# First FFN split in two parts, with Strassen's scheme for 19 of its 22 tiles

## The chip, the cores and the metric

The kernel runs on one core of one Trainium2 chip. The metric is device time in microseconds (us), the median of several runs. Engines are named as in the profile: PE (TensorE), DVE (VectorE), ACT (ScalarE), POOL (GpSimd), SP (SyncE, which here only issues transfers).

## The reference

One layer over 512 latent tokens and 256 context tokens, model width 1024, in float32. Nine vectors of modulation per token kind come from one product with `w_mod`. FFN 1 (both token kinds), attention with pooling, and FFN 2 (latent tokens alone) follow each other.

```python
def swiglu(h, w_gu, w_down):
    a, b = jnp.split(h @ w_gu, 2, axis=-1)        # width 2 x 2816
    return (jax.nn.silu(a) * b) @ w_down
...
    ml = jnp.split(mod_lat, N_MOD, axis=-1)       # silu(c) @ w_mod + b_mod
    lat = lat + 0.5 * ml[2] * swiglu(modulate(rms_norm(lat, g_norm[layer, 0]), ml[0], ml[1]),
                                     w_ffn_gu[layer, 0], w_ffn_down[layer, 0])
    cx = cx + 0.5 * mc[2] * swiglu(modulate(rms_norm(cx, g_norm[layer, 0]), mc[0], mc[1]),
                                   w_ffn_gu[layer, 0], w_ffn_down[layer, 0])
...
    lat = lat + ml[5] * branch_merge(attn_lat, pool_lat, gates_l, ...)
    lat = lat + 0.5 * ml[8] * swiglu(modulate(rms_norm(lat, g_norm[layer, 2]), ml[6], ml[7]),
                                     w_ffn_gu[layer, 1], w_ffn_down[layer, 1])
return rms_norm(lat, g_final)
```

## The kernel before

**Products.** Every float32 operand is kept as a high and a low part (`split`, L121 on ACT and L122 on DVE). A product is three matmuls (`mm3`): high times high (L138), high times low (L139), low times high (L141). A weight tile of 128 x 1024 is loaded by SP (`weights`), split, and used from a ring of four.

**FFN 1.** The hidden width 2816 is 22 tiles of 128 (j). `Hidden` makes one tile: gate and up, each over 8 blocks of 128 input rows (kt), for 512 latent and 256 context columns. ACT applies Silu, DVE multiplies gate and up (L407), and the product is split and stays on chip. After each group of tiles (`CHUNKS`: 4, 4, 4, 4, 2, 4) `ffn_down` projects the group back: for each of 8 output blocks i, the tiles of the group are multiplied into two PSUM banks, and DVE adds the result to the residual streams xo and xc (L544). So gate, up and down alternate. There are 7 PSUM banks in a ring and one for the totals below.

**Modulations.** Vectors 0 and 1 are needed at the start. `Mod` makes vectors 2 to 8 beside FFN 1: for each block kt of the condition, `step` loads rows of `wm` on POOL's queue (1 MB for two blocks, two buffers) and DVE adds them, scaled, to an accumulator macc (L250; the first by L252). The vectors 2 to 4 have two accumulators, one for each token kind, 5 to 8 one. `total` sums over the partitions by matmuls on PE (acc, L260), and `finish` brings the vector into place. The steps are handed out between the tiles.

**FFN 2** has 4 plain tiles and 18 tiles by Strassen's scheme: `Quad` takes gate and up of one tile as a 2 x 2 block product over two halves of 4 kt and two halves of 256 tokens, in seven products of 4 kt instead of eight. The sums of weight blocks are made by DVE (L450, L451) and POOL (L453, L454), and split. `HalfSums` makes the four sums of token blocks once, t0 to t3, one for each pair of kt (POOL adds high and low, L509; DVE differences, L513).

**Order.** The program is written as if it ran in sequence. A scheduler sets the order of the instructions on each engine; each engine then runs its own queue in order, and semaphores hold an instruction until its inputs are there.

Of the kernel before, what the change touches and what calls it, by code (L numbers as in the profile page):

```python
# [97 lines left out]
def tile_layer(ctx: ExitStack, tc: tile.TileContext, a: dict, out: bass.AP):  # L98
# [259 lines left out]
    hl = [hp.tile([P, 2, SEQ], F32R, name=f"hl{k}") for k in range(KT)]  # L358
    def stream_tile():
        t = xo.tile([P, KT, SEQ], F32, name="xo")  # L360
        return t, [t[:, k, :] for k in range(KT)]

    xl_all, xl = stream_tile()
    hctx_stack = ExitStack()
    hcp = pool("hcp", hctx_stack, bufs=1, side="right")
    HCW = CTX + 8
    hc_new = lambda: [hcp.tile([P, 2, HCW], F32R, name=f"hc{k}")[:, :, 0:CTX] for k in range(KT)]
    hc = hc_new()
# [870 lines left out]
```

## Time and profile before

| | us |
|---|---|
| median of 3 runs | 1494.99 (1494.97 to 1495.32) |
| the profiled execution, its own time | 1496.38 |
| its span | 1494.6 |
| PE busy | 1458.3 |
| DVE busy | 951.1 |
| ACT busy | 602.1 |
| POOL busy | 327.9 |

The span is the time from the first to the last instruction of the profiled execution. The busy times are sums over the whole span; the stretches differ from each other: FFN 1 runs to about 580 us, FFN 2 begins at about 1130 us. The granted clock of PE is 0.997 of full speed over the span.

### The profile page before, as it was taken

How to read it: one execution, taken by the hardware profiler on the slowest of the kernel's cores; microseconds unless marked ns; L12 is line 12 of the kernel's file. 1: busy time of each engine (PE TensorE's matmuls, PEld its weight loads, DVE VectorE, ACT ScalarE, POOL GpSimd, SP SyncE). 2: the span in 40 equal slices, each digit the busy share in tenths (PEclk: the TensorE clock that was granted, in tenths of full speed). 3: DMA queues.
4: the chain of work that ended last, by engine and by line, in shares of the span. 5: the costliest groups of instructions: out<-in, count | busy, mean ns of one | idle time of the engine just before them, and what ended most of it. 6: DMA issues, size and time to landing. Idle time of an engine off the chain costs nothing.

```text
span 1494.6 us, 22635 instructions
## 1 busy us (share of the span) xinstructions
PE 1458.3 (98%) x9280; PEld 1301.5 (87%) x9280; DVE 951.1 (64%) x1423; ACT 602.1 (40%) x989; POOL 327.9 (22%) x239
## 2 busy tenths in 40 slices
PE   6999999999999999989999999999999999999998
PEld 4888888888888889979999988888899799989997
DVE  5678468433233237677767677633487978879786
ACT  5321121221221225666666666422356434434343
POOL 1000001000000013544545555000144422212210
PEclk9999999999999999999999999999999999999999
DMA  9445368312112122310101111433353323233231
GB/s 377 163 156 183 113 226 280 129 57 71 57 57 73 37 64 71 128 57 29 57 30 57 35 66 50 141 99 92 106 169 120 93 85 113 86 113 114 85 99 57
DMA packets 41497, 156.69 MB, mean 105 GB/s; under 512 B 4657, under 2 KB 4913, under 8 KB 37425
## 3 DMA queue, kind: packets, MB, share of 16 engines
q1 hardware_dynamic: 36640, 124.76, 25.4%
q0 software_dynamic: 4032, 29.36, 5.4%
q8 instruction: 73, 1.20, 0.3%
q10 hardware_dynamic: 720, 1.11, 0.2%
q14 instruction: 32, 0.25, 0.1%
HBM read 151.03 MB, written 4.19 MB: 104 GB/s over the span
## 4 chain that ended last, share of the span: by engine, by line
PE 87%; DVE 7%; ACT 2%; issue 2%; POOL 1%; DMA 0%; DVEq 0%; SPq 0%; ACTq 0%; POOLq 0%
PE ps L138 26%; PE ps L139 26%; PE ps L141 26%; PE sc L877 1%; PE sc L876 1%; PE ps L901 1%; PE ps L785 1%; PE ps L786 1%; PE ps L787 1%; DVE w_lo L122 1%; DVE tmp L301 1%; DVE tmp L323 1%; DVE e L887 1%; DVE tmp L513 1%; ACT w_hi L121 1%
## 5 line engine op out<-in xcount | busy, mean ns | idle before, releaser
L121 ACT ACTIVATE w_hi<-w_raw 128x1024 fp32r<-128x1024 f32 (+1 forms) x213 | 210.2, 988 | 591.2 <-PE ps L139 317.8
L138 PE MATMUL ps<-hl,w_hi 128*128 128x512 f32 (+1 forms) x880 | 324.8, 372 | 0.8 <-DVE xo L913 0.4
L139 PE MATMUL ps<-hl,w_hi 128*128 128x512 f32 (+1 forms) x880 | 322.1, 367 | 0.0
L141 PE MATMUL ps<-hl,w_lo 128*128 128x512 f32 (+1 forms) x880 | 321.8, 367 | 0.0
L122 DVE TENSOR_TENSOR w_lo<-w_raw,w_hi 128x1024 fp32r<-128x1024 f32 (+1 forms) x175 | 210.3, 1202 | 133.9 <-ACT w_hi L121 133.2
L122 POOL TENSOR_TENSOR w_lo<-w_raw,w_hi 128x1024 fp32r<-128x1024 f32 x38 | 93.0, 2449 | 504.8 <-ACT w_hi L121 474.0
L138 PE MATMUL ps<-act_hi,w_hi 128*128 128x512 f32 (+1 forms) x592 | 200.7, 339 | 0.1
L139 PE MATMUL ps<-act_lo,w_hi 128*128 128x512 f32 (+1 forms) x592 | 192.3, 335 | 0.0
L138 PEld LDWEIGHTS ps<-hl,w_hi 128*128 128x128 f32 x880 | 165.6, 189 | 29.7 <-issue 2.2
L141 PEld LDWEIGHTS ps<-hl,w_lo 128*128 128x128 f32 x880 | 165.8, 189 | 13.5 <-issue 0.4
L139 PEld LDWEIGHTS ps<-hl,w_hi 128*128 128x128 f32 x880 | 166.1, 189 | 11.6 <-DVE hl L330 0.3
L141 PE MATMUL ps<-act_hi,w_lo 128*128 128x512 f32 (+1 forms) x592 | 174.0, 337 | 1.6 <-DVE w_lo L122 1.6
L139 PE MATMUL ps<-hc,w_hi 128*128 128x256 f32 (+1 forms) x484 | 136.5, 282 | 0.0
L141 PE MATMUL ps<-hc,w_lo 128*128 128x256 f32 (+1 forms) x484 | 135.6, 281 | 0.0
L138 PE MATMUL ps<-hc,w_hi 128*128 128x256 f32 (+1 forms) x484 | 135.6, 282 | 0.0
L138 PEld LDWEIGHTS ps<-act_hi,w_hi 128*128 128x128 f32 x592 | 111.7, 189 | 19.2 <-issue 0.8
L139 PEld LDWEIGHTS ps<-act_lo,w_hi 128*128 128x128 f32 x592 | 111.8, 189 | 11.9
L544 DVE SCALAR_TENSOR_TENSOR xo<-ps,mods,xo 128x512 f32<-128x512 f32 (+1 forms) x112 | 74.3, 670 | 70.2 <-PE ps L141 70.1
L141 PEld LDWEIGHTS ps<-act_hi,w_lo 128*128 128x128 f32 x592 | 102.3, 190 | 8.7 <-DVE w_lo L122 3.1
L138 PEld LDWEIGHTS ps<-hc,w_hi 128*128 128x128 f32 x484 | 90.7, 188 | 16.5 <-ACT hc L329 0.2
L139 PEld LDWEIGHTS ps<-hc,w_hi 128*128 128x128 f32 x484 | 91.1, 188 | 15.6 <-issue 0.2
L250 DVE SCALAR_TENSOR_TENSOR macc<-wm,cond,macc 128x1024 f32<-128x1024 f32 x70 | 88.7, 1280 | 6.8 <-DMA wm<-in_wm 6.1
(252 smaller groups left out, 2847.1 us busy)
## 6 DMA issues: line engine op xcount, KB each, us to landing
w_raw<-in_gu SPq DMA_DIRECT2D x88, 512.0 KB, 3.5
wm<-in_wm POOLq DMA_DIRECT2D x28, 1024.0 KB, 5.2
w_raw<-in_dn SPq DMA_DIRECT2D x40, 512.0 KB, 3.6
w_raw<-in_wi SPq DMA_DIRECT2D x36, 512.0 KB, 3.5
wm<-in_wm SPq DMA_DIRECT2D x16, 512.0 KB, 10.9
w_raw<-in_wo SPq DMA_DIRECT2D x16, 512.0 KB, 3.5
w_raw<-in_wv SPq DMA_DIRECT2D x8, 512.0 KB, 3.5
w_raw<-in_wa SPq DMA_DIRECT2D x8, 512.0 KB, 3.4
```

The lines of the kernel that those rows point to most:

```text
L121: nc.scalar.activation(out=hi, in_=src, func=AF.Copy)
L122: (lo_engine or nc.vector).tensor_tensor(out=lo, in0=src, in1=f32(hi), op=ALU.subtract)
L138: nc.tensor.matmul(out=o, lhsT=wh, rhs=ah, start=start, stop=False)
L139: nc.tensor.matmul(out=o, lhsT=wh, rhs=al, start=False, stop=False)
L141: nc.tensor.matmul(out=o, lhsT=wl, rhs=ah, start=False, stop=stop)
L250: nc.vector.scalar_tensor_tensor(out=acc, in0=wm, scalar=c, in1=acc, op0=ALU.mult, op1=ALU.add)
L301: nc.vector.tensor_tensor(out=acc, in0=acc, in1=sq, op=ALU.add)
L323: nc.vector.scalar_tensor_tensor(out=t, in0=x, scalar=scale, in1=r, op0=ALU.mult, op1=ALU.mult)
L513: sub = lambda out, x, y, op=ALU.subtract: nc.vector.tensor_tensor(out=out, in0=x, in1=y, op=op)
L544: nc.vector.scalar_tensor_tensor(out=xa, in0=po, scalar=mod(gate_i, i, s), in1=xa, op0=ALU.mult, op1=ALU.add)
L785: nc.tensor.matmul(out=o, lhsT=hh, rhs=vh, start=(kt == 0), stop=False)
L786: nc.tensor.matmul(out=o, lhsT=hh, rhs=vl, start=False, stop=False)
```

## The change

- The first three tiles of FFN 1 (`PLAIN1`) stay plain, with two spans of 384 columns instead of 512 and 256. Latent and context tokens lie side by side in one tile of 768 columns (hb).
- Tiles 3 to 21 are `Quad`s over halves of 384 tokens, with `HalfSums` over hb. The weight sums have two buffers instead of the three of FFN 2.
- The product of gate and up of every tile, 128 x 768, goes to DRAM (`store_act`, on POOL's queue). After the last quad the pools of this part are closed; x and the context are loaded again (8 transfers of SP).
- Then `ffn_down` runs for groups of 2, 5, 8, 3 and 4 tiles (`ACT_CHUNKS`). Their activations come back through `Stored`: one load by SP, and a split into two tiles. The group of two is loaded during the last quads.
- A step of `Mod` loads 512 KB for one kt instead of 1 MB for two. Modulations 2 to 4 run beside the quads, with one wm buffer; their steps are called twice in each quad. Modulations 5 to 8 run beside the down projections, two steps for each output block, with two wm buffers.

```diff
 CHUNKS = (4, 4, 4, 4, 2, 4)
+ACT_CHUNKS = (2, 5, 8, 3, 4)
+PLAIN1 = 3
...
         def step(self, kt):
-            if kt % 2 == 0:
-                self.wm = self.pool.tile([P, 2, D], F32, name="wm")
-                if self.after is not None:
-                    nc.gpsimd.tensor_copy(out=self.wm[:, 0, 0:1], in_=self.after)
-                nc.gpsimd.dma_start(out=self.wm, in_=a["wm"][self.i - 2, kt // 2])
+            wm = self.pool.tile([P, D], F32, name="wm")
+            nc.gpsimd.dma_start(out=wm, in_=a["wm"][self.i - 2, kt // 2, :, kt % 2])
             if kt == 0:
-                self.acc = [self.pool.tile([P, D], F32, name="macc", bufs=3) for _ in self.streams]
+                self.acc = [self.pool.tile([P, D], F32, name="macc", bufs=2) for _ in self.streams]
...
+    class Stored:
...
+            raw = raw_pool.tile([P, ALL], F32, name="act_raw")
+            nc.sync.dma_start(out=raw, in_=src)
...
+            split(lat_tile[:, 0, :], lat_tile[:, 1, :], raw[:, 0:SEQ])
+            split(ctx_tile[:, 0, :], ctx_tile[:, 1, :], raw[:, SEQ:ALL])
...
-    both = [(hl, 0, SEQ), (hc, 0, CTX)]
+    HALF = ALL // 2
+    both = [(hb, 0, HALF), (hb, HALF, HALF)]
...
+    def store_act(j, gate):
+        nc.gpsimd.dma_start(out=act_dram[j], in_=gate)
...
+    modp1 = pool("modp1", right_stack, bufs=1, side="right")
...
+    sums1 = HalfSums(hb, HALF, tq1, row)
+    quads1 = {j: Quad(w_gu1, j, wq1, 2, cq1, sums1, row, lambda q, gate: store_act(q.j, gate)) for j in range(PLAIN1, NJ)}
...
+    todo = [lambda k=k: sums1.build(k) for k in range(HK)]
+    for h_ in first[2:]:
+        for part in range(2):
+            h_.products(part, range(KT // 2))
+            if todo:
+                todo.pop(0)()
...
+    def add_mods(idx, pool_):
+        for i in idx:
+            m = Mod(i, pool_, (LAT, CX) if i < 5 else (LAT,))
+            pending.extend([lambda m=m, kt=kt: m.step(kt) for kt in range(KT)] + [m.total, m.finish])
...
+    add_mods((2, 3, 4), modp1)
+    stored = []
+    for j, qd in quads1.items():
+        qd.all(next_pending)
...
+    for k in range(0, KT, 2):
+        nc.sync.dma_start(out=xl_all[:, k:k + 2], in_=a["xT"][:, k:k + 2])
+        nc.sync.dma_start(out=xc_all[:, k:k + 2], in_=a["cT"][:, k:k + 2])
...
+    modp = pool("modp", ffn_stack, bufs=2)
+    add_mods((5, 6, 7, 8), modp)
...
+    two = lambda: (next_pending(), next_pending())
...
+        following = bring(starts[c + 1], nj, c + 1 != 2)
+        run(ffn_down(w_dn1, starts[c], acts, every), {i: two for i in range(KT)})
+        acts = following
```

Two places in the order of the instructions. The first is DVE while the third tile of FFN 1 and its neighbours are on PE. Before, the steps of modulation 2 (macc) stand between low parts of weights (w_lo) and of activations (act_lo):

```order
L250 SCALAR_TENSOR_TENSOR macc_716<-wm_722,cond_83,macc_716 128x1024
L250 SCALAR_TENSOR_TENSOR macc_717<-wm_722,cond_83,macc_717 128x1024
L122 TENSOR_TENSOR w_lo_923<-w_raw_921,w_hi_922 128x1024
L122 TENSOR_TENSOR act_lo_702<-tmp_703,act_hi_701 128x512
L122 TENSOR_TENSOR act_lo_702<-tmp_708,act_hi_701 128x256
L250 SCALAR_TENSOR_TENSOR macc_716<-wm_853,cond_83,macc_716 128x1024
L250 SCALAR_TENSOR_TENSOR macc_717<-wm_853,cond_83,macc_717 128x1024
L122 TENSOR_TENSOR w_lo_993<-w_raw_991,w_hi_992 128x1024
L250 SCALAR_TENSOR_TENSOR macc_716<-wm_853,cond_83,macc_716 128x1024
L250 SCALAR_TENSOR_TENSOR macc_717<-wm_853,cond_83,macc_717 128x1024
L250 SCALAR_TENSOR_TENSOR macc_716<-wm_916,cond_83,macc_716 128x1024
L407 TENSOR_TENSOR tmp_843<-tmp_843,ps_791 128x512
```

After the change the same stretch of DVE's queue is the end of the block sums: differences (gate from up, L516), steps of modulation 2 (macc_1002, macc_1003) and the low parts of t2 and t3, on which the first quad's matmuls wait.

```order
L516 TENSOR_TENSOR gate_847<-up_845,gate_847 128x384
L249 SCALAR_TENSOR_TENSOR macc_1003<-wm_1317,cond_74,macc_1003 128x1024
L516 TENSOR_TENSOR gate_848<-up_845,gate_847 128x384
L124 TENSOR_TENSOR t2_657<-gate_847,t2_657 128x768
L516 TENSOR_TENSOR gate_885<-up_881 128x384
L124 TENSOR_TENSOR t2_657<-gate_848,t2_657 128x768
L516 TENSOR_TENSOR gate_885<-up_883,gate_885 128x384
L516 TENSOR_TENSOR gate_886<-up_881,up_883 128x384
L249 SCALAR_TENSOR_TENSOR macc_1002<-wm_1425,cond_74,macc_1002 128x1024
L249 SCALAR_TENSOR_TENSOR macc_1003<-wm_1425,cond_74,macc_1003 128x1024
L516 TENSOR_TENSOR gate_886<-up_883,gate_885 128x384
L124 TENSOR_TENSOR t3_658<-gate_885,t3_658 128x768
```

The steps of modulation 2 have moved in between the block sums.

The second is the total of modulation 5. On PE before, it stands between two tiles of gate and up (ps from hl and hc):

```order
L139 MATMUL ps_2352<-hl7_110,w_hi_2347 128x512
L138 MATMUL ps_2353<-hc7_122,w_hi_2347 128x256
L139 MATMUL ps_2353<-hc7_122,w_hi_2347 128x256
L141 MATMUL ps_2352<-hl7_110,w_lo_2348 128x512
L141 MATMUL ps_2353<-hc7_122,w_lo_2348 128x256
L260 MATMUL acc_2402<-macc_2083,half_100 32x256 x4
L138 MATMUL ps_2415<-hl0_103,w_hi_2410 128x512
L139 MATMUL ps_2415<-hl0_103,w_hi_2410 128x512
```

On DVE its last step (macc_2083) stands in a piece between low parts, some tiles ahead:

```order
L122 TENSOR_TENSOR w_lo_1955<-w_raw_1953,w_hi_1954 128x1024
L250 SCALAR_TENSOR_TENSOR macc_2083<-wm_2148,cond_83,macc_2083 128x1024 x2
L250 SCALAR_TENSOR_TENSOR macc_2083<-wm_2270,cond_83,macc_2083 128x1024 x2
L407 TENSOR_TENSOR tmp_1796<-tmp_1796,ps_1744 128x512
L407 TENSOR_TENSOR tmp_1801<-tmp_1801,ps_1745 128x256
L122 TENSOR_TENSOR w_lo_2021<-w_raw_2019,w_hi_2020 128x1024
L122 TENSOR_TENSOR act_lo_1795<-tmp_1796,act_hi_1794 128x512
L122 TENSOR_TENSOR act_lo_1795<-tmp_1801,act_hi_1794 128x256
L250 SCALAR_TENSOR_TENSOR macc_2083<-wm_2342,cond_83,macc_2083 128x1024 x2
L122 TENSOR_TENSOR w_lo_2088<-w_raw_2086,w_hi_2087 128x1024
```

After the change the total (acc_3793) stands on PE between output blocks of the first down group (act_a are its two activations):

```order
L143 MATMUL ps_3778<-act_a_3076,w_lo_3773 128x256
L140 MATMUL ps_3778<-act_a_3083,w_hi_3772 128x256
L141 MATMUL ps_3778<-act_a_3083,w_hi_3772 128x256
L143 MATMUL ps_3778<-act_a_3083,w_lo_3773 128x256
L259 MATMUL acc_3793<-macc_3694,half_91 32x256 x4
L268 MATMUL ps_3800<-ident_63,tmp_3798 128x4 x2
L140 MATMUL ps_3804<-act_a_3076,w_hi_3772 128x512
L141 MATMUL ps_3804<-act_a_3076,w_hi_3772 128x512
```

On DVE the steps of modulation 5 (macc_3694) stand in front of the residual update of the next output block (L563, ps_3804), the first three of modulation 6 (macc_3822) too:

```order
L249 SCALAR_TENSOR_TENSOR macc_3694<-wm_3715,cond_74,macc_3694 128x1024
L249 SCALAR_TENSOR_TENSOR macc_3694<-wm_3718,cond_74,macc_3694 128x1024
L124 TENSOR_TENSOR hl1_3890<-act_raw_3892,hl1_3890 128x512
L249 SCALAR_TENSOR_TENSOR macc_3694<-wm_3743,cond_74,macc_3694 128x1024
L249 SCALAR_TENSOR_TENSOR macc_3694<-wm_3746,cond_74,macc_3694 128x1024
L249 SCALAR_TENSOR_TENSOR macc_3694<-wm_3765,cond_74,macc_3694 128x1024
L249 SCALAR_TENSOR_TENSOR macc_3694<-wm_3768,cond_74,macc_3694 128x1024
L251 TENSOR_SCALAR macc_3822<-wm_3820,cond_74 128x1024
L271 TENSOR_TENSOR mods_90<-ps_3800,vecs_64 128x8
L249 SCALAR_TENSOR_TENSOR macc_3822<-wm_3824,cond_74,macc_3822 128x1024
L249 SCALAR_TENSOR_TENSOR macc_3822<-wm_3849,cond_74,macc_3822 128x1024
L563 SCALAR_TENSOR_TENSOR xo_3616<-ps_3804,mods_90,xo_3616 128x512
```

On POOL the loads of these steps follow the last activation stores:

```order
L649 DMA act20_219<-gate_3382 128x768
L649 DMA act21_220<-gate_3489 128x768
L243 DMA wm_3692<-in_wm 128x1024
L243 DMA wm_3696<-in_wm 128x1024
L243 DMA wm_3715<-in_wm 128x1024
L243 DMA wm_3718<-in_wm 128x1024
```

The last step, the total and the down projections behind it now stand within one group.

## Rows read from the trace of the kernel before

**Rows 1.** The page: busy time, GB/s by fortieth, chain that ended last
```profile
PE 1458.3 (98%) x9280; PEld 1301.5 (87%) x9280; DVE 951.1 (64%) x1423; ACT 602.1 (40%) x989; POOL 327.9 (22%) x239
...
GB/s 377 163 156 183 113 226 280 129 57 71 57 57 73 37 64 71 128 57 29 57 30 57 35 66 50 141 99 92 106 169 120 93 85 113 86 113 114 85 99 57
...
PE 87%; DVE 7%; ACT 2%; issue 2%; POOL 1%; DMA 0%; DVEq 0%; SPq 0%; ACTq 0%; POOLq 0%
```

**Rows 2.** Busy us by stretch: length, PE, PEld, DVE, ACT, POOL, clock, DMA, GB/s
```profile
30.00:120.00 90.00, 90.00 (x605) 75.29 (x604) 62.40 (x83) 28.73 (x45) 8.19 (x12) 1.00 0.54 193
120.00:400.00 280.00, 280.00 (x1634) 241.70 (x1634) 151.06 (x187) 52.08 (x78) 10.55 (x20) 1.00 0.40 138
...
1147.00:1185.00 38.00, 36.40 (x216) 32.23 (x215) 37.53 (x49) 18.75 (x31) 17.93 (x9) 1.00 0.26 84
...
1200.00:1480.00 280.00, 279.90 (x1986) 263.61 (x1986) 237.39 (x343) 114.79 (x153) 56.59 (x32) 1.00 0.30 95
```

**Rows 3.** Timeline of PE near 704 us: start, us, instruction
```profile
704.08 0.34 PE L876 MATMUL sc<-k,q 128*128 128x384 f32 x1
704.25 0.33 PE L877 MATMUL sc<-k,ql 128*128 128x384 f32 x1
704.42 0.33 PE L876 MATMUL sc<-k,q 128*128 128x384 f32 x1
704.60 0.28 PE L138 MATMUL ps<-pa_hi,v_hi 128*128 128x256 f32 x1
704.72 0.28 PE L139 MATMUL ps<-pa_lo,v_hi 128*128 128x256 f32 x1
```

**Rows 4.** Timeline of DVE near 55 us: last normalised block of FFN 1
```profile
54.44 0.74 DVE L330 SCALAR_TENSOR_TENSOR hl<-tmp,mods,hl 128x512 fp32r<-128x512 f32 x1
55.10 0.47 DVE L330 SCALAR_TENSOR_TENSOR hc<-tmp,mods,hc 128x256 fp32r<-128x256 f32 x1
```

**Rows 5.** DVE by line and form: count, busy us, mean ns, idle before
```profile
L122 DVE TENSOR_TENSOR w_lo<-w_raw,w_hi 128x1024 fp32r<-128x1024 f32 x140 | 185.9, 1328 | 118.8 <-ACT w_hi L121 118.3
L250 DVE SCALAR_TENSOR_TENSOR macc<-wm,cond,macc 128x1024 f32<-128x1024 f32 x70 | 88.7, 1280 | 6.8 <-DMA wm<-in_wm 6.1
...
L122 DVE TENSOR_TENSOR w_lo<-w_raw,w_hi 128x512 fp32r<-128x512 f32 x35 | 24.4, 697 | 15.1 <-ACT w_hi L121 14.9
...
L475 DVE TENSOR_TENSOR tmp<-u,ps 128x256 f32<-128x256 f32 x36 | 13.5, 416 | 5.6 <-PE ps L141 5.1
...
L450 DVE TENSOR_TENSOR s<-w_raw 128x512 f32<-128x512 f32 x18 | 12.4, 687 | 15.3 <-DMA w_raw<-in_gu 15.3
...
L486 DVE TENSOR_TENSOR tmp<-tmp 128x512 f32<-128x512 f32 x18 | 12.3, 681 | 0.5 <-ACT tmp L484 0.4
...
L252 DVE TENSOR_SCALAR macc<-wm,cond 128x1024 f32<-128x1024 f32 x10 | 7.4, 749 | 11.1 <-PE acc L260 6.0 <-issue 4.5 <-DMA wm<-in_wm 0.7
```

**Rows 6.** Timeline of DVE, block sums of FFN 2
```profile
1150.11 0.42 DVE L513 TENSOR_TENSOR tmp<-tmp 128x256 f32<-128x256 f32 x1
1150.45 1.22 DVE L122 TENSOR_TENSOR w_lo<-w_raw,w_hi 128x1024 fp32r<-128x1024 f32 x1
...
1157.11 0.41 DVE L122 TENSOR_TENSOR act_lo<-tmp,act_hi 128x256 fp32r<-128x256 f32 x1
1157.44 1.52 DVE L513 TENSOR_TENSOR tmp<-tmp 128x256 f32<-128x256 f32 x1
...
1164.17 2.31 DVE L122 TENSOR_TENSOR w_lo<-w_raw,w_hi 128x1024 fp32r<-128x1024 f32 x1
...
1180.10 0.68 DVE L122 TENSOR_TENSOR t<-tmp,t 128x512 fp32r<-128x512 f32 x1
```

**Rows 7.** Timeline of POOL in the same place
```profile
1157.26 2.86 POOL L509 TENSOR_TENSOR tmp<-hl 128x512 f32<-128x512 f32 x2 [3.77 <-DVE tmp L513]
...
1163.79 3.84 POOL L509 TENSOR_TENSOR tmp<-hl 128x512 f32<-128x512 f32 x2 [1.03 <-DVE tmp L513]
```

**Rows 8.** Waits of PE, 1140 to 1490 us: for what, us, times, longest
```profile
PE ps L141 <- DVE w_lo L122: 1.6, 1, 1.6
PE ps L139 <- DVE t L122: 1.5, 1, 1.5
```

**Rows 9.** DMA issues, 100:560 us, then 0:60 us: KB, median us to landing
```profile
w_raw<-in_gu SPq DMA_DIRECT2D x34, 512.0 KB, 3.5
w_raw<-in_dn SPq DMA_DIRECT2D x4, 256.0 KB, 2.7
...
wm<-in_wm SPq DMA_DIRECT2D x16, 512.0 KB, 10.9
```

**Rows 10.** POOL by line: wm load, count, busy us, mean ns, idle before
```profile
L244 POOL DMA_DIRECT2D wm<-in_wm x28 | 15.0, 535 | 199.7 <-DVE macc L250 188.7 <-DVE mods L292 10.4 <-POOL wm L243 0.6
```

**Rows 11.** Line 260, totals: what PE waited for before them
```profile
its engine sat idle before it (us, times) until:
  issue: 1.7, 7
```

More of the change, by code (lines that the diff above doesn't have):

```diff
@@ L355, in inserts @@
             return r
[L358 to L368, printed above, removed]
+    ALL = SEQ + CTX
+    first_stack = ExitStack()
+    hb_pool = pool("hb", first_stack, bufs=1)
+    hb = [hb_pool.tile([P, 2, ALL], F32R, name=f"hb{k}") for k in range(KT)]
+    hl_view = [t[:, :, 0:SEQ] for t in hb]
+    hc_view = [t[:, :, SEQ:ALL] for t in hb]
     def h_act(h, kt, t0, t1):
@@ L471, in all @@
                 self.following.prepare()
[L472 to L474 removed]
+            n = self.sums.n
+            t0, t1 = slice(0, n), slice(n, 2 * n)
+            gate, up = self.rows("gate"), self.rows("up")
+            p1, u2, u4 = (self.cpool.tile([P, n], F32, name=i) for i in ("p1", "u2", "u4"))
             add = lambda out, x, ps, op=ALU.add: nc.vector.tensor_tensor(out=out, in0=x, in1=ps, op=op)
@@ L697, in tile_layer @@
-    norm_last = []
-    ffn_chunks(lambda j: Hidden(w_gu1, j, actp, both), w_dn1, [(0, SEQ, xl, 0, 2, LAT), (SEQ, CTX, xc, 0, 2, CX)],
-               first, between, lambda *p: norm_last.append(last1(*p)))
+    todo = [lambda k=k: sums1.build(k) for k in range(HK)]
[4 more added lines that the diff above has]
+                todo.pop(0)()
+            h_.products(part, range(KT // 2, KT))
+            if todo:
+                todo.pop(0)()
+        h_.close()
@@ new lines, in tile_layer, with stream_tile @@
+    assert stored
+    gate_vec(2)
+    scale_vec(4, 1)
+    first_stack.close()
+    ring["tmp"] = pool("tmp", bufs=8)
+    hp = pool("hp", bufs=1)
+    xo = pool("xo", bufs=1)
+    def stream_tile():
+        t = xo.tile([P, KT, SEQ], F32, name="xo")
+        return t, [t[:, k, :] for k in range(KT)]
+    ffn_stack = ExitStack()
+    xcp = pool("xcp", ffn_stack, bufs=1)
+    xl_all, xl = stream_tile()
+    xc_all = xcp.tile([P, KT, CTX], F32, name="xc")
+    xc = [xc_all[:, k, :] for k in range(KT)]
@@ new lines, in bring @@
+    def bring(j0, n, own):
+        got = []
+        for k in range(n):
+            if own:
+                t = actp.tile([P, 2, ALL], F32R, name="act")
+                lt, ct = t[:, :, 0:SEQ], t[:, :, SEQ:ALL]
+            else:
+                lt = hp.tile([P, 2, SEQ], F32R, name=f"hl{k}")
+                ct = hcp.tile([P, 2, HCW], F32R, name=f"hc{k}")[:, :, 0:CTX]
+            got.append(Stored(act_dram[j0 + k], rawp, lt, ct))
+        return got
+    every = [(0, SEQ, xl, 0, 2, LAT), (SEQ, CTX, xc, 0, 2, CX)]
@@ L1103, in tile_layer, with split_act @@
     cq = pool("cq", quad_stack, bufs=2)
-    sums = HalfSums(hl, tq)
-    quads = {j: Quad(w_gu2, j, ap2, wq, cq, sums.y) for j in range(PLAIN, NJ)}
+    sums = HalfSums(hl, SEQ // 2, tq, lambda name: scratch(SEQ))
+    def split_act(q, gate):
+        q.hi = ap2.tile([P, SEQ], F32R, name="act_hi")
+        q.lo = ap2.tile([P, SEQ], F32R, name="act_lo")
+        split(q.hi, q.lo, gate)
+    quads = {j: Quad(w_gu2, j, wq, 3, cq, sums, lambda name: scratch(SEQ), split_act) for j in range(PLAIN, NJ)}
     for j, qd in quads.items():
```

188 lines of the change are left out of this document (109 added, 79 removed).

## The prediction

> **What bounds the kernel now.** The page comes first: PE is busy 1458.3 of 1494.6 us and holds 87% of the chain that ended last [rows 1]. The average hides stages, so the windows come next. In the first FFN (FFN 1) PE is busy in 280.00 of 280 us and DVE in only 151.06. In FFN 2, which runs Strassen's scheme already, PE is still full at 279.90 of 280, but DVE has risen to 237.39. Only where FFN 2 builds its block sums does PE lose some time: 1.6 of 38 us, with DVE busy 37.53 [rows 2]. So each matmul column taken out of FFN 1 is worth its time, as long as DVE, POOL and the transfers keep PE's queue fed. That queue runs in order: one matmul that waits holds all behind it. The totals of the modulation (the acc matmuls) stand in it as well; before the change PE idled 1.7 us in all ahead of them, for nothing that the trace names [rows 11].
>
> **What is removed.** A plain tile is 48 pairs of a 512 and a 256 column matmul. 1634 matmuls in 280.00 us [rows 2] make 0.3427 us a pair and 16.45 us a tile. A quad is 84 matmuls of 384 columns. Two such follow each other at 0.17 to 0.18 us [rows 3]; halfway between 512 and 256 columns the pair gives 0.171. I take 0.1725, so 14.5 us a quad. 19 tiles save 19 x (16.45 - 14.5) = 37 us, 33 to 39 by 0.175 and 0.1714. The three plain tiles go from 48 pairs to 96 matmuls of 384, at most 0.4 us more. The columns of the down projections don't change. Gain taken: 36.6.
>
> **The block sums come late.** Quad 3 needs t0 to t3. Work on them can begin when the last normalised block is there, at 55.6 us [rows 4]. From there to the last t3 split DVE's queue holds: 12 mod steps at 1.28 and 2 at 0.75 (16.9), 6 low parts of weights of 1024 elements at 1.22 and 2 of 512 at 0.70 (8.7), 4 weight sums at 0.68 (2.7), 16 differences of 384 and 4 gate products of 384, between 0.42 and 0.68, taken as 0.55 (11), and 8 low parts of 768 at 0.95 (7.6) [rows 5, 6]. This is 47 us of durations. Successive ones overlap by about 0.08, as the two instructions at 1150.11 and 1150.45 show [rows 6], which leaves 43. POOL's sums run in the same stretch and slow DVE: a 256 column difference took 1.52 instead of 0.42 while POOL added, a low part 2.31 instead of 1.22 [rows 6, 7], so 1.1 us for a POOL sum of 512. There are 8 sums of 768 (1.6 each) and 4 of 512: 17 us. So t3 is done at 55.6 + 43 + 17 = 116 us. PE has less: from 55.6 some 6 to 10 us of tiles 0 and 1, the third plain tile (96 x 0.1725 = 16.6), 12 matmuls of p1 and 27 on t0 to t2 (6.7), and is through at 90. What else quad 3 could do (p2, p3) waits for PSUM banks that only the gate of tile 2 frees, and that gate stands behind t3 on DVE. The wait is 116 - 90 = 26. Without POOL's interference it is 9, with half of it 17; scaling FFN 2's own stage of 30.7 us (1150.1 to 1180.8, [rows 6]) by 1.5 and adding the mod steps puts t3 at 119, a wait of 29. I take 24, bounds 14 to 32. FFN 2 paid 1.5 us in the like place, a wait for t [rows 8]: it has no mod steps there, and four plain tiles to hide behind instead of three.
>
> The Trainium skill (GPSIMD Engine Reference, Specifications) says that GpSimd's interface to the on-chip memory is shared with VectorE, and that instructions with two inputs there contend. The differences and low parts are such, and rows 6 and 7 agree; the gate products, with one input in PSUM, would escape it. By that rule the stage would be at most 2 us shorter.
>
> **Quads that carry mod steps.** A quad costs DVE 7 additions from PSUM at 0.55, a product of 768 at 0.95, 2 weight sums at 0.68, 3 low parts at 1.22 and one at 0.70, 10.5 in durations and 9.6 after overlap; POOL's two sums add 2.2 [rows 5 to 7]. 11.8 is under PE's 14.5, so plain quads hold PE full, as FFN 2 does with 85% on DVE. Eight quads (four for each of two modulations) carry two mod steps with two streams each, 4 x 1.2 = 4.8 more: 16.6, two over PE. Of 8 x 2 = 16 the queue's slack takes part in the first quads of each four. I take 8, bounds 0 to 16.
>
> **The modulations in the down stage.** Call T the end of the last quad's last matmul. Modulations 5 to 8 are 32 loads of 512 KB with two buffers, on POOL's queue behind the last activation store. That store waits for two DVE instructions (0.55 and 0.95), and issuing takes 0.535 [rows 10]; the second load also waits for the stores to land, 2.7 us and more [rows 9]. At the same time x and the context come back, 3 MB, which at 377 GB/s [rows 1] is 8 us; loads in such a crowd took 10.9 [rows 9]. On DVE the first step also stands behind the residual update of output block 4 and four splits. So steps 1 and 2 run at T + 14 to 16.5. Each further pair needs an issue, a landing of 3.5 and an update of 1.28 [rows 5, 9, 10]: 5.3 us, three times, T + 32. PE does five output blocks of the first chunk (6 pairs each, 2.06 us, to T + 10.3), and then its queue holds the total of modulation 5. It waits 22 us, and 16 to 27 by landings of 2.7 to 5. Behind it, on PE, stand all further down projections. Modulation 6 follows at the same pace, to T + 54 to 59; PE, back at T + 32.5, loses 3 to 4 us because three steps of modulation 6 stand on DVE ahead of the update that frees a bank, and reaches the next total at T + 53: together 8 more (2 to 12). Modulations 7 and 8 need 22 us each, and PE has 20 to 26 and 38 us of matmuls between: nothing. Term: 30, bounds 18 to 39. Before, these loads waited 188.7 us for free buffers [rows 10], and it cost nothing, since the total stood far behind them.
>
> The Trainium skill (DMA: Bandwidth & Descriptors, Anatomy of one DMA) prices a transfer from GpSimd at 2.0 us plus bytes at 436 GB/s, so 3.2 for 512 KB; this estimate would take 1 us off the first wait. No row here has a 512 KB load on that queue.
>
> The stores (22 of 384 KB) and their reloads lie beside PE and are charged nothing; if a reload came late, the chunk would wait one landing, about 3.5. The steps from the last down chunk on keep their order.
>
> **Sum.** The profiled run took 1496.4 us, 1.4 more than the median. 1496.4 - 36.6 + 24 + 8 + 30 = 1521.8, as a median 1520. With all lower bounds it is 1488, with all upper ones 1548.
>
> **The rivals.** (1) Forecast: all three losses, 1500 to 1546, slower. Its decisive mechanism is the 5.3 us round of two buffers: from a round of about 2 us on, the down stage would hide it. (2) The block sums hide as in FFN 2 (2 us instead of 24): 1498. For it speaks that FFN 2 does it, against it that DVE was full in that stage and now has 16.9 us more. (3) The loads of modulations 5 to 8 hold PE for 5 us only: 1495. This needs landings well under the 2.7 of a 256 KB load. (4) Neither wait bites and only the quads lose: 1495 - 36.6 + 8 + 2 + 5 = 1473, and 1460 if nothing is lost. For it speaks that before the change PE never waited in this stretch. (5) The waits grow on each other: POOL's in-order queue holds wm loads that wait for DVE ahead of the weight sums of the next quad, on all 19 quads: 3 us more on ten of them, 1550.
>
> **How the numbers follow.** Chances: (1) 0.70, (2) 0.09, (3) 0.06, (4) 0.09, (5) 0.06. Within 0.2% is 3 us, about what a measurement can tell. Faster takes (4), half of (3) and a little of (2): 0.14. Same takes the rest of (3), half of (2): 0.08. Slower: 0.78. The range leaves out (4), the top of (5) and the outer edges of (1): 1488 to 1545.
>
> **What would show it.** In PE's waits: one of 14 to 32 us for a DVE split of t near 90 us, and one of 16 to 27 us for the 8th macc step of modulation 5 near 390 us, ahead of an acc total, with DVE idle for the wm loads in that stretch. The quads should show a matmul pitch of 0.1725 and PE full where no mod steps run. Wrong would be a PE at 100% across either place, or wm landings under 2 us.

## The result

| | us |
|---|---|
| before, median of 4 runs | 1495.15 (1494.97 to 1495.9) |
| changed, median of 4 runs | 1538.66 (1537.25 to 1540.57) |
| ratio | 1.0291 [1.0273, 1.0309] |
| predicted | 1520 (1488 to 1545) |

The change is slower by 43.5 us. That is the forecast sign, inside the range, and 18.7 us above the predicted value. The page of the changed kernel, in the places of [rows 1]: busy times, the granted clock in 40 slices, the chain.

```profile
PE 1437.3 (93%) x9052; PEld 1315.1 (85%) x9052; DVE 1118.0 (73%) x1625; ACT 650.2 (42%) x1038; POOL 431.5 (28%) x331
...
PEclk9969999999868999999999999999999999999999
...
PE 59%; DVE 10%; issue 4%; DMA 4%; ACT 2%; POOL 1%; DVEq 0%; ACTq 0%; POOLq 0%
```

PE's busy time fell by 21.0 us (1458.3 to 1437.3), but its span grew by 44.2. Its share of the chain went from 87% to 59%, and transfers of wm stand in the chain now. The clock row, which was 9 throughout, drops in the third slice (77 to 115 us) and in the 11th to 13th (385 to 500 us): both places come back below. The waits of PE over the whole run (what for, us, times, longest) name the places; of the waits for t, nine with 18.2 us lie in the block sums of FFN 1:

```profile
PE acc L259 <- DVE macc L249: 41.4, 3, 32.3
...
PE ps L141 <- DVE t L124: 9.9, 6, 3.9
PE ps L140 <- ACT t L123: 9.8, 4, 4.3
```

Before, the totals of the modulation waited for nothing [rows 11], and the block sums of FFN 2 cost one wait of 1.5 us [rows 8]. The busy time by stretch, columns as in [rows 2]; the first is the block sums, the second the quads behind the first one, the third the down projections, the last a part of the quads:

```profile
85.00:127.00 42.00, 23.87 (x90) 19.50 (x90) 41.01 (x44) 10.28 (x14) 16.47 (x12) 0.63 0.29 97
127.00:399.00 272.00, 271.82 (x1572) 264.94 (x1571) 236.10 (x291) 91.54 (x114) 71.69 (x67) 1.00 0.38 123
399.00:648.00 249.00, 204.06 (x1233) 179.71 (x1232) 145.95 (x227) 67.01 (x124) 38.21 (x51) 0.89 0.52 169
200.00:260.00 60.00, 60.00 (x353) 58.52 (x352) 58.66 (x72) 20.80 (x25) 19.16 (x18) 1.00 0.47 151
```

All of the difference lies in FFN 1. From the first matmul of FFN 1 to the last residual update it took 579.4 us before (24.96 to 604.4, so FFN 1 ends later than the 580 us named further up) and 622.4 after (25.4 to 647.8); attention begins 43.7 us later than before and the rest has the same length.

**The block sums.** On PE, start, duration and instruction, with the wait in brackets:

```profile
88.82 0.34 PE L140 MATMUL ps<-t,wq_hi 128*128 128x384 f32 x1
93.06 0.69 PE L141 MATMUL ps<-t,wq_hi 128*128 128x384 f32 x1 [3.90 <-DVE t L124]
...
100.90 0.52 PE L141 MATMUL ps<-t,wq_hi 128*128 128x384 f32 x1
101.22 0.52 PE L143 MATMUL ps<-t,wq_lo 128*128 128x384 f32 x1
...
123.47 0.33 PE L141 MATMUL ps<-hb,wq_hi 128*128 128x384 f32 x1
123.65 0.33 PE L143 MATMUL ps<-hb,wq_lo 128*128 128x384 f32 x1
```

The third plain tile and what the first quad could do with the first half of t0 ended at 89.2 us; the second half of t0 and then t1 to t3 came one after the other. From there PE got its matmuls in small groups. Between them it idled and its granted clock fell: in 92 to 96 us it was 0.50, the lower of its two levels (1.2 of 2.4 GHz), and the matmuls of 384 columns at 100.90 and 101.22 stand 0.32 us apart instead of the 0.17 and 0.18 at 123.47. DVE wrote the last part of t3 at this time:

```profile
116.27 1.94 DVE L124 TENSOR_TENSOR t<-gate,t 128x768 fp32r<-128x768 f32 x2
```

The quad ended at 126.9. Begun at 85.7 and with 84 x 0.1735 = 14.6 us of matmuls it would have ended at 100.3: it cost 26.6 us more. The nine waits are 18.2 us of it, none longer than 4.3. Most of the other 8.4 is the lower clock: 36 matmuls begin between 93 and 121.6 us, at 0.32 us each or more instead of 0.17, which is 5 us or more.

**The down stage.** The last quad's last matmul begins at 399.11. First POOL, then DVE, then PE:

```profile
401.83 0.54 POOL L649 DMA_DIRECT2D act<-gate  x1 [14.02 <-DVE gate L491]
402.37 0.54 POOL L243 DMA_DIRECT2D wm<-in_wm  x1
411.13 0.54 POOL L243 DMA_DIRECT2D wm<-in_wm  x1 [8.23 <-DMA act<-gate]
```

```profile
420.24 0.75 DVE L251 TENSOR_SCALAR macc<-wm,cond 128x1024 f32<-128x1024 f32 x1
421.02 1.28 DVE L249 SCALAR_TENSOR_TENSOR macc<-wm,cond,macc 128x1024 f32<-128x1024 f32 x1
...
427.10 2.61 DVE L249 SCALAR_TENSOR_TENSOR macc<-wm,cond,macc 128x1024 f32<-128x1024 f32 x2 [1.58 <-DMA wm<-in_wm]
...
432.61 1.28 DVE L249 SCALAR_TENSOR_TENSOR macc<-wm,cond,macc 128x1024 f32<-128x1024 f32 x1 [1.96 <-DMA wm<-in_wm]
435.15 1.28 DVE L249 SCALAR_TENSOR_TENSOR macc<-wm,cond,macc 128x1024 f32<-128x1024 f32 x1 [1.26 <-DMA wm<-in_wm]
438.29 1.29 DVE L249 SCALAR_TENSOR_TENSOR macc<-wm,cond,macc 128x1024 f32<-128x1024 f32 x1 [1.86 <-DMA wm<-in_wm]
440.83 1.28 DVE L249 SCALAR_TENSOR_TENSOR macc<-wm,cond,macc 128x1024 f32<-128x1024 f32 x1 [1.25 <-DMA wm<-in_wm]
```

```profile
442.17 1.08 PE L259 MATMUL acc<-macc,half 128*32 128x256 f32 x8 [32.31 <-DVE macc L249]
```

The last activation store was issued at 401.83, and the second wm load could go only at 411.13, when that store had landed. The first step ran at 420.24. Its load was not what it waited for last: the trace has the first wm load landed at 412.8 and the second at 418.3. Ahead of it in DVE's queue stood four splits of activations for the next group, whose loads, issued at 405.9 in the crowd of x and context, took 11.6 us (first ACT, then DVE):

```profile
417.44 0.94 ACT L123 ACTIVATE act<-act_raw 128x512 fp32r<-128x512 f32 x2 [8.96 <-DMA act_raw<-act]
...
418.11 1.03 DVE L124 TENSOR_TENSOR act<-act_raw,act 128x512 fp32r<-128x512 f32 x2 [4.16 <-ACT act L123]
```

From 420.24 on each pair of steps took 5.5 to 6.9 us, and the eighth ended at 442.1. PE had been waiting since 409.9. The transfers of this place (KB, median us to landing; compare [rows 9]):

```profile
wm<-in_wm POOLq DMA_DIRECT2D x20, 512.0 KB, 4.8
...
xo<-in_xT SPq DMA_DIRECT2D x4, 512.0 KB, 10.7
...
act<-gate POOLq DMA_DIRECT2D x1, 384.0 KB, 8.6
```

**The quads** with two steps were full on PE: 60.00 us of 60 in the last stretch of the table above, with DVE at 58.66. Copies of the first product by ACT, one for each quad, show their pace:

```profile
175.30 0.49 ACT L479 ACTIVATE p<-ps 128x384 f32<-128x384 f32 x1 [1.50 <-PE ps L143]
...
192.31 0.49 ACT L479 ACTIVATE p<-ps 128x384 f32<-128x384 f32 x1
...
206.85 0.49 ACT L479 ACTIVATE p<-ps 128x384 f32<-128x384 f32 x1 [1.67 <-PE ps L143]
...
221.41 0.49 ACT L479 ACTIVATE p<-ps 128x384 f32<-128x384 f32 x1 [1.67 <-PE ps L143]
...
235.97 0.49 ACT L479 ACTIVATE p<-ps 128x384 f32<-128x384 f32 x1 [1.67 <-PE ps L143]
```

Quads of the mod steps take 14.56 us (206.85 to 221.41, 221.41 to 235.97). The one from 175.30 takes 17.0: its queue holds the matmuls of a total between its own, of which a pair by itself costs 0.8 us (15.34 in place of 14.56 for each of the three quads ahead of it).

### The profile page after: what moved, and what is told of

It reads as the page before. It is cut to its first block, busy times and chain, and to the rows that moved or that the text cites. A ratio compares the mean times of both kernels' runs of the same rounds, so it can differ in the third digit from the quotient of the medians.

```text
span 1538.8 us, 22802 instructions
## 1 busy us (share of the span) xinstructions
PE 1437.3 (93%) x9052; PEld 1315.1 (85%) x9052; DVE 1118.0 (73%) x1625; ACT 650.2 (42%) x1038; POOL 431.5 (28%) x331
## 4 chain that ended last, share of the span: by engine, by line
PE 59%; DVE 10%; issue 4%; DMA 4%; ACT 2%; POOL 1%; DVEq 0%; ACTq 0%; POOLq 0%
PE ps L140 17%; PE ps L143 17%; PE ps L141 17%; DMA wm<-in_wm 3%; DVE w_lo L124 1%; PE sc L983 1%; PE sc L982 1%; PE ps L1007 1%; DVE macc L249 1%; PE ps L891 1%; PE ps L892 1%; PE ps L893 1%; DMA act_raw<-act 1%; ACT w_hi L123 1%; DVE wq_lo L124 1%
## 5 line engine op out<-in xcount | busy, mean ns | idle before, releaser
L123 ACT ACTIVATE w_hi<-w_raw 128x1024 fp32r<-128x1024 f32 (+3 forms) x217 | 202.5, 935 | 345.2 <-PE ps L141 304.6
L124 DVE TENSOR_TENSOR w_lo<-w_raw,w_hi 128x1024 fp32r<-128x1024 f32 (+3 forms) x179 | 211.9, 1184 | 50.8 <-ACT w_hi L123 50.5
L140 PE MATMUL ps<-hl,w_hi 128*128 128x512 f32 (+1 forms) x592 | 209.9, 357 | 0.7 <-DVE xo L1019 0.4
L141 PE MATMUL ps<-hl,w_hi 128*128 128x512 f32 (+1 forms) x592 | 208.4, 354 | 0.0
L143 PE MATMUL ps<-hl,w_lo 128*128 128x512 f32 (+1 forms) x592 | 208.0, 354 | 0.0
L140 PE MATMUL ps<-t,wq_hi 128*128 128x384 f32 (+1 forms) x444 | 140.2, 317 | 9.8 <-ACT t L123 9.8
L141 PE MATMUL ps<-t,wq_hi 128*128 128x384 f32 (+1 forms) x444 | 140.0, 315 | 9.9 <-DVE t L124 9.9
L143 PE MATMUL ps<-t,wq_lo 128*128 128x384 f32 (+1 forms) x444 | 137.7, 314 | 0.3 <-DVE wq_lo L124 0.2
L140 PEld LDWEIGHTS ps<-hl,w_hi 128*128 128x128 f32 x592 | 111.6, 189 | 15.0 <-DVE xo L1019 0.6
L141 PEld LDWEIGHTS ps<-hl,w_hi 128*128 128x128 f32 x592 | 111.9, 189 | 10.9
L563 DVE SCALAR_TENSOR_TENSOR xo<-ps,mods,xo 128x512 f32<-128x512 f32 (+1 forms) x104 | 68.2, 663 | 68.6 <-PE ps L143 67.5
L124 DVE TENSOR_TENSOR wq_lo<-s,wq_hi 128x1024 fp32r<-128x1024 f32 x74 | 108.5, 1467 | 1.5 <-ACT wq_hi L123 1.5
L140 PEld LDWEIGHTS ps<-t,wq_hi 128*128 128x128 f32 x444 | 85.0, 192 | 15.5 <-ACT t L123 11.8
L141 PEld LDWEIGHTS ps<-t,wq_hi 128*128 128x128 f32 x444 | 85.3, 192 | 12.4 <-DVE t L124 12.4
L143 PEld LDWEIGHTS ps<-t,wq_lo 128*128 128x128 f32 x444 | 85.4, 193 | 0.9 <-DVE wq_lo L124 0.8
```

Source lines behind the costliest of these rows:

```text
L123: nc.scalar.activation(out=hi, in_=src, func=AF.Copy)
L124: (lo_engine or nc.vector).tensor_tensor(out=lo, in0=src, in1=f32(hi), op=ALU.subtract)
L140: nc.tensor.matmul(out=o, lhsT=wh, rhs=ah, start=start, stop=False)
L141: nc.tensor.matmul(out=o, lhsT=wh, rhs=al, start=False, stop=False)
L143: nc.tensor.matmul(out=o, lhsT=wl, rhs=ah, start=False, stop=stop)
L563: nc.vector.scalar_tensor_tensor(out=xa, in0=po, scalar=mod(gate_i, i, s), in1=xa, op0=ALU.mult, op1=ALU.add)
```

## The experiments

The theory to test: PE's queue lost its time at two places, behind the block sums and behind the totals of modulations 5 to 8, with a lower clock after each. The rivals are a crowd of transfers that would hold PE anyway, POOL's pace, and an overload of DVE in the quads.

**e1_no58.** The edit:

```diff
-            m = Mod(i, pool_, (LAT, CX) if i < 5 else (LAT,))
+            if i >= 5:
+                pending.append(lambda i=i: bias_only(i, 1))
+                continue
```

> Leaves out modulations 5 to 8 (their loads, DVE steps and totals; the vectors are the bias alone). Theory 1: the down stage loses its time only because PE's queue holds their totals, and PE's lower clock after each wait is part of that price. Then the stage from the last quad (399.5 us) to the last residual update (647.8) shrinks from 248 to 195 to 202 us, PE's clock there stays at 1.0, and the time is 1486 to 1494. Theory 2: the crowd of transfers at that place (x, context, activations, weights) is the limit, and PE would wait for an activation or a weight instead: 1515 or more, with a wait of PE of over 15 us for a split of act or w.

1484.0 us (1483.5 to 1485.6), ratio to before 0.9931 [0.9916, 0.9946]: 54.7 us less than the changed kernel. The down stage now (columns as in [rows 2]):

```profile
399.00:591.00 192.00, 190.50 (x1186) 170.91 (x1185) 107.73 (x189) 65.50 (x120) 21.21 (x19) 1.00 0.42 131
```

PE is busy 190.5 of 192 us, at full clock. x, the context, the activations and the weights come through the same crowd, and nothing on PE waits for them: theory 1, with 1484.0 two us below its band and a stage of 191.4 us (399.3 to 590.7) below its 195. So the crowd by itself costs PE nothing. With the mod steps in place it does cost something, since the splits that wait for it stand ahead of them on DVE.

**e2_no24.** The same edit for `i < 5`, with both token kinds.

> Leaves out modulations 2 to 4 (bias alone); 5 to 8 stay. Theory 1: the block sums are late because DVE carries too much: 14 of the mod instructions (16.9 us) stand ahead of t3. Then t3 is done at 101 to 104 us instead of 118, the first quad ends 12 to 16 us earlier, the three totals inside the quads give 5 to 9 us more, and the time is 1512 to 1522. Theory 2: POOL's sums, which wait on DVE and DVE on them, set the pace of the block sums: t3 moves by less than 6 us, time 1525 or more.

1512.6 us (1512.4 to 1514.1), ratio 1.0123 [1.0108, 1.0138], 26.1 less. The last write of t3 begins at 104.41 instead of 116.27:

```profile
104.41 1.90 DVE L124 TENSOR_TENSOR t<-gate,t 128x768 fp32r<-128x768 f32 x2
```

On PE the first quad took 30.3 us (85.1 to 115.3) where it had taken 41.2, and all others 14.56. The time is in the band of theory 1, t3 (done at 106.3) and the end of the first quad (11.6 us earlier) fall just short of its numbers. So the steps of modulation 2 are worth about 11 us of the block sums, and the totals and steps in the quads about 10; the rest was won in the down stage. Some 16 us of loss remain in the first quad without any mod step: the sums alone are too much for three plain tiles.

**e3_nopool.** The edit, in `HalfSums.build`:

```diff
                 hi, lo = h_act(self.h, kt, 0, 2 * n)
+                if n == HALF:
+                    y.append(f32(hi))
+                    continue
```

> Leaves out the low parts in the block sums of the first FFN, and with them the 8 additions of 768 on POOL; the mod steps stay. Theory 1: POOL's additions stretch DVE's instructions by 1.1 us per 512 columns, so 8 x 1.6 = 13 us: t3 at 103 to 107 us, time 1522 to 1528. Theory 2: the chain of single buffered wm loads (landing about 4.5, then two steps of DVE) sets the pace, since t3 stands behind the seventh step: t3 at 113 or later, time 1533 or more.

1524.6 us (1524.1 to 1528.4), ratio 1.0206 [1.0191, 1.0222], 14.0 less than the changed kernel, with the last write of t3 at 109.15. The time is that of theory 1, t3 lies between the two: 7 us earlier where 11 to 15 were expected. PE's waits for t are 10.4 us in place of 18.2, and the last quad ends 8.7 us earlier (390.6 against 399.3). The rest came later and was not followed further. The edit also moved other work: all 16 instructions of modulation 2's steps now stand ahead of the end of t3, where 14 did, DVE waited 3.4 us for wm loads among them, which is theory 2's chain, and the total of modulation 2 stands inside the first quad (107.6 to 111.5). So POOL's sums are a part of the delay, but this run doesn't give their share alone.

**e4_spread.** The steps and totals by output block (c is the down group, i the block):

```diff
+        if c == 1:
+            late[5].step(i)
+        if c == 2:
+            m = late[6 if i < 4 else 7]
+            for kt in (2 * (i % 4), 2 * (i % 4) + 1):
+                m.step(kt)
+        if c == 3:
+            late[8].step(i)
+        if (c, i) in ((2, 1), (2, 6), (3, 3)):
+            m = late[{(2, 1): 5, (2, 6): 6, (3, 3): 7}[c, i]]
+            m.total()
+            m.finish()
```

> Complete computation. Modulations 5 to 8 start with the second down group instead of the first (one step per output block there, two in the group of eight, one in the group of three), and each total stands two or more output blocks behind its last step; the last one inside the last group. Theory 1: only the place of the totals in PE's queue costs time; the loads themselves hide: no wait of PE for macc over 1 us, time 1488 to 1497. Theory 2: the crowd of transfers is the limit: PE waits as long for activations or weights, 1515 or more.

1497.9 us (median of 10; 1495.3 to 1503.2), ratio 1.0028 [1.0015, 1.0040]: 40.8 less, 0.9 above the band of theory 1. All 32 loads and steps are still there. The waits for macc are gone, but there is a new one, since finish stands right behind its total on PE and waits for ACT's copy of it:

```profile
PE ps L268 <- ACT tmp L262: 8.9, 4, 5.4
```

So it is where the totals and the steps stand that costs, and not the amount of loads; the steps moved too, behind the reload of x, so the run doesn't tell the two places apart. Of e1's 54.7 us the spreading gives back 40.8.

**e5_fix3.** Two edits: finish some blocks behind its total, and the first load of modulation 2 waits for t3:

```diff
+            if self.after is not None and kt == 0:
+                nc.gpsimd.tensor_copy(out=wm[:, 0:1], in_=self.after)
             nc.gpsimd.dma_start(out=wm, in_=a["wm"][self.i - 2, kt // 2, :, kt % 2])
```

> Complete computation. Two edits together: the first step of modulation 2 waits for the last low part of t3, so that no mod step stands among the block sums; and modulations 5 to 8 as in e4_spread, with the finish of each some output blocks behind its total. Theory 1: t3 is done at 104 to 108 us as in e2_no24, the first quad loses 12 instead of 27 us, and the down stage 5 to 8 instead of about 53: 1470 to 1480. Theory 2: the moved steps overload DVE in the quads instead, where it was 98% busy already: quads with steps take over 15.5 us, time 1483 or more.

1492.7 us (median of 10; 1488.5 to 1496.7), ratio 0.9980 [0.9967, 0.9994]. The number falls to theory 2, but only in small part for its reason: PE's waits for low parts and additions of DVE in the quads are 3.4 us. The first quad did a little better than in e2_no24, 28.1 us (85.1 to 113.2), and the down stage had no stall left. PE lost its time at the total of modulation 2, whose steps had become later than its place:

```profile
176.50 3.15 PE L261 MATMUL acc<-macc,half 128*32 128x256 f32 x16 [9.11 <-DVE macc L251]
```

It is the same mechanism as in the down stage, moved to the quads.

**e6_fix4 and e7_fix5.** e5_fix3 with `PLAIN1 = 4` and `PLAIN1 = 5`.

> Complete computation. As e5_fix3, with four plain tiles and 18 quads. The fourth plain tile costs 16.7 instead of 14.6 us and gives PE 16.7 us of work while the block sums are made. Theory 1: the 12 us that the first quad still lost go to 0 to 4, net 6 to 10 us less than e5_fix3: 1462 to 1472. Theory 2: the block sums are pushed back by the fourth tile's own work on DVE (about 6 us) and POOL's: wait of 5 us or more, no gain over e5_fix3 beyond 4 us.

> Complete computation. As e6_fix4, with five plain tiles and 17 quads. Theory 1: nothing is left to hide, so only the dearer tile shows: 2 us more than e6_fix4. Theory 2: if e6_fix4 still waits for the block sums, this is 2 us or more below it.

1480.9 us (1479.6 to 1482.5), ratio 0.9906 [0.9889, 0.9922], and 1480.0 (1478.1 to 1481.9), ratio 0.9896 [0.9882, 0.9911]. Both forecasts missed: e6 is 9 us above theory 1, and e7 is neither 2 us above nor 2 below e6. In e6 PE waits once for 10.3 us, for a Silu of a plain tile:

```profile
PE ps L140 <- ACT gate L406: 10.3, 1, 10.3
```

```profile
105.01 1.78 ACT L123 ACTIVATE t<-gate 128x768 fp32r<-128x768 f32 x2 [3.44 <-DVE gate L518]
...
107.64 1.61 ACT L406 ACTIVATE gate<-ps 128x384 f32<-128x384 f32 x4
```

ACT does this Silu (L406) behind the high parts of t3. The block sums and the plain tiles share two rows named gate, so the Silu of the third tile has no row to write into before t3 is done; its PSUM banks stay taken, and the fourth tile can't go on. In e7 this wait is 8.8 us; e10 below, with rows of their own, doesn't have it.

**e9_fix3_own and e10_fix4_own.** The block sums get rows of their own, from the accumulators that modulation 2 uses afterwards; modulation 2 then needs no wait of its own. The down stage is as in e5_fix3; e10 has `PLAIN1 = 4`.

```diff
+    sums_row = lambda name: modp1.tile([P, D], F32, name="macc", bufs=2)[:, 0:ALL] if name == "so" else row(name)
-    sums1 = HalfSums(hb, HALF, tq1, row)
+    sums1 = HalfSums(hb, HALF, tq1, sums_row)
...
-            o = [self.rows("gate") for _ in range(2)]
+            o = [self.rows("so" if n == HALF else "gate") for _ in range(2)]
```

> Complete computation. Modulations 5 to 8 as in e5_fix3. The block sums take their scratch rows from the two accumulator buffers of the modulations instead of the two gate rows that the plain tiles use. Modulation 2 so begins behind the sums, without a wait of its own, and the last plain tile can be closed ahead of t3. Theory 1: the gate rows were one of the two chains that held the first quad: t3 at 98 to 102 us, wait of the first quad under 8 us, 3 to 8 us less than e5_fix3. Theory 2: DVE's and POOL's work alone sets t3: within 2 us of e5_fix3.

> Complete computation. As e9_fix3_own with four plain tiles. In e6_fix4 PE waited 10.3 us for the Silu of the third plain tile, which waited for a gate row that the block sums held until 107 us. Theory 1: with rows of their own that wait is under 2 us, PE's clock stays at 1.0 there, 1465 to 1473. Theory 2: it becomes a wait for t3 of the same length: 1478 to 1482.

e9: 1476.4 us (1474.8 to 1476.7), ratio 0.9869 [0.9854, 0.9883], the best of all and below both kernels. The last write of t3 begins at 96.01:

```profile
96.01 0.95 DVE L124 TENSOR_TENSOR t<-macc,t 128x768 fp32r<-128x768 f32 x1
```

On PE the first quad takes 21.5 us (86.6 to 108.1), 6.9 more than its matmuls, with waits for t of 4.2 and 0.6. It ends 5.0 us earlier than in e5, as theory 1 had it. The whole run gains 16.3 on e5 and not 3 to 8, since in the quads behind it the wait of 9.1 for the total of modulation 2 is down to 0.9 as well.

e10: 1477.9 us (1476.1 to 1481.6), ratio 0.9884 [0.9869, 0.9899], outside theory 1 and at the edge of theory 2, but with neither's wait: none for the Silu and none for t. PE lost 9 us in 110 to 135, where DVE's queue held mod steps whose loads had not landed, ahead of a weight's low part and of an addition that frees a bank:

```profile
104.06 2.48 DVE L249 SCALAR_TENSOR_TENSOR macc<-wm,cond,macc 128x1024 f32<-128x1024 f32 x2 [4.13 <-DMA wm<-in_wm]
...
111.44 2.48 DVE L249 SCALAR_TENSOR_TENSOR macc<-wm,cond,macc 128x1024 f32<-128x1024 f32 x2 [3.76 <-DMA wm<-in_wm]
...
120.46 2.48 DVE L249 SCALAR_TENSOR_TENSOR macc<-wm,cond,macc 128x1024 f32<-128x1024 f32 x2 [5.01 <-DMA wm<-in_wm]
```

So with three plain tiles, rows of their own and the mod steps behind them the sums cost 6.9 us in place of 26.6; the fourth tile buys nothing.

**e12_own.** The block sums of e9 alone, modulations 5 to 8 as in the changed kernel.

> Complete computation. The block sums alone as in e9_fix3_own (rows of their own, modulation 2 behind them); modulations 5 to 8 as in the changed kernel. Theory 1: the two losses add up: e9_fix3_own ended the first quad at about 111 instead of 127 us, so 14 to 22 us less than the changed kernel, 1517 to 1525, and PE still waits over 25 us for the total of modulation 5. Theory 2: what is won in front is given back behind, since modulations 2 to 4 then fill DVE in the quads: 1530 or more.

1519.1 us (1518.9 to 1520.2), ratio 1.0165 [1.0148, 1.0181], 19.5 less than the changed kernel, with 33.3 us of wait for the total of modulation 5 still there. The first quad ends at 108.0, 18.9 earlier. So the first loss goes without touching the second. From here the spreading of modulations 5 to 8 gives another 42.7 (e12 to e9), and both edits together 62.2 (1538.7 to 1476.4); in e4, with the first loss still there and the finish right behind each total, it gave 40.8.

**e8_warm and e11_warm2.** The clock. Extra matmuls, whose result nothing reads, ahead of the total of modulation 5 (135 in e8, though its expectation says 131, then 146):

```diff
+            if self.i == 5:
+                hot = stored[0].lat[:, 0, :]
+                filler = ps_m.tile([P, 512], F32, name="acc")
+                for _ in range(146):
+                    nc.tensor.matmul(out=filler, lhsT=hot[:, 0:P], rhs=hot, start=True, stop=True)
```

> As the changed kernel, with 131 extra matmuls of 512 columns, whose result nothing reads, ahead of the total of modulation 5; 125 of them stand at the place where PE waits 32.3 us, and take about 28.5. Theory 1: the lower clock after the wait is a cost of its own, some 3 us there: with PE kept busy the granted clock in the 10 us behind the wait is 1.0 instead of 0.5 to 0.55, and the time is 1533 to 1537. Theory 2: the clock is low there for another reason than PE's idling: it stays at 0.5, and the time is 1538 to 1542.

> As e8_warm with 15 more of the extra matmuls, so that they reach past the end of the wait, where e8_warm still left 3.0 us of idling and a lower clock behind it. Theory 1: idling, even 3 us of it, lowers the clock: without any the granted clock stays at 1.0 through 455 us, and the down projections behind the total start at once at full pitch; time 1533 to 1537. Theory 2: the clock falls at the small matmuls of the total itself: it reads 0.5 to 0.6 there again.

1535.8 us both (1535.1 to 1537.5 and 1534.2 to 1537.8), ratios 1.0271 [1.0256, 1.0286] and 1.0272 [1.0255, 1.0289]. The time is that of theory 1, the clock is not. In e8 3.0 us of idling were left, and the clock was at 0.56 in 445 to 450, as without the extra work. In e11 0.9 us were left before the total and 0.5 before its finish; PE's busy us and granted clock around them:

```profile
441.00:443.00 2.00, 1.65 (x8) 1.00 0.43 139
443.00:445.00 2.00, 0.99 (x11) 1.00 0.53 166
445.00:447.00 2.00, 2.00 (x10) 0.64 0.74 252
447.00:449.00 2.00, 2.00 (x8) 0.51 0.66 213
449.00:451.00 2.00, 2.00 (x13) 1.00 0.22 74
```

It was 1.00 through the wait, fell behind the total all the same, and was 1.00 again in 449 to 451. So neither run shows PE's full clock behind a total, and which of the short idles and the small matmuls brings it down stays open. The 2.9 us that both won can't be put down to the clock: PE's waits for the later totals also fell, from 9.1 us to 6.5 in e8 and 3.1 in e11, and why they did stays open.

## Why the prediction was right, and where it was off

The sign and the two places were right: t3 was late by DVE's queue, and the total of modulation 5 held PE's queue while wm loads went round in two buffers. The sizes; the second and third rows are what the quads took beyond 14.57 us each, the last is the whole difference that e1 makes:

| term | predicted | measured |
|---|---|---|
| saving of 19 quads and 3 plain tiles | -36.6 | -43.4 |
| block sums, first quad | +24 | +26.6 |
| 18 quads behind it | +8 | +10.1, of which about 5 were paid before too (three totals at 1.1 and 0.5) |
| modulations in the down stage | +30 | +54.7 (e1_no58) |

The measured saving: matmul starts of the kernel before at 300.17 and 311.74 enclose 33 pairs, 0.3506 us each, so 16.83 a tile; 19 x (16.83 - 14.57) = 42.9, and 0.5 for the plain tiles. The column adds up to 48.0. About 9 us of it, the seven totals' own matmuls, were paid before too; that leaves 39 of the 43.5, and the other 4 or 5 were not followed. The forecast's own upper bounds add up to 1549 and not 1548, which changes nothing.

**Removed work: mis-sized.** The 0.3427 us for a pair came from all 1634 matmuls of a window [rows 2]; those include the short ones of the totals, which the step overlooked. The pitch for 384 columns was right (0.1735 against 0.1725).

**Block sums: the cause right, the size near in part by luck.** PE stopped at 89.2 (forecast 90) and t3 came at 118.2 (forecast 116). But the forecast was one wait of 14 to 32 us with t0 to t2 in place, and the run has nine, none above 4.3 and 18.2 in all, since t0 to t2 came late too. What made up the rest is the clock, which the step did not name: 36 matmuls at 0.32 us or more instead of 0.17. Its two parts, mod steps and POOL's interference, show in e2 and e3, where t3 comes 11.9 and 7.2 us earlier; they had been put at 16.9 and 17. It also took the banks' wait for t3 as given; e6 and e9 show that the shared gate rows were behind it.

**Quads: the amount near, the reason wrong.** DVE was not over PE's time. 200 to 260 us hold 12 mod instructions in about four quads, three each and not four, since a total and its finish take two of the ten turns of a modulation. Additions with an input in PSUM ran at 0.54 to 0.55 us beside POOL. The Trainium skill's rule that VectorE instructions with two inputs in the on-chip memory contend with GpSimd (GPSIMD Engine Reference, Specifications) agrees with this stretch: the low parts of sums took 1.34 us on the mean and the products of gate and up 1.61, in place of 1.21 and 0.95, the additions nothing more. The 10.1 us are totals whose matmuls stand singly between others.

**Down stage: mis-sized, 30 for 55.** The mechanism was that of the forecast: loads through two buffers, and a total that holds PE's queue. The term that failed is the landings in the crowd. The first step was put at T + 14 to 16.5 and ran at T + 20.8 (T, the end of the last quad, is 399.4). The prediction named the four splits that stand ahead of it on DVE; their loads took 11.6 us, and that set the time. The last store was late as well (8.6 us, taken: 2.7), but the second load behind it landed at T + 18.9, before the splits were done. The rounds took 5.5 to 6.9 us instead of 5.3, since a wm load took 4.8 and not 3.5. The wait of 22 became 32.3. The estimate from the Trainium skill (DMA: Bandwidth & Descriptors, Anatomy of one DMA), 3.2 us for 512 KB, is lower than the 4.8 of this place and the 4.5 of the whole run; the measurement decides. The waits of 6.9 and 2.2 for the next two totals fit the 8 that were given for them. The rest was not in the sum at all: after each of the three waits PE ran below full clock (31 matmuls in 443 to 451, where 58 had fit into 10 us before the wait: 2.6 us at 0.17 each), it waited 2.0 us for ACT's copies, and e1 leaves out the totals' own matmuls, some 1.2 us each at full clock (0.7 and 0.5 before), which were paid before too. No run gives these loads more buffers or another place for the reload of x, so the shares of the two are not separated.

**Rivals.** (2) and (3) are refuted by the waits. (4) is what e9 comes to: with the waits for the totals nearly gone and 6.9 us left in the first quad the time is 1476, near its 1473. (5) did not show: PE waited 0.2 us for a low part of the weight sums in the whole run.
